# The modulation vectors of a hybrid block: column groups of TensorE in place of VectorE products

## The chip, the cores and the metric

The kernel runs on one core of one Trainium2 chip. The metric is the device time of one execution in microseconds (us); three executions of the kernel before took 2481.51 to 2481.74 us, with a median of 2481.51.

## The reference

One block of a transformer-like model works on 2048 latent tokens of 1024 features and on 256 context tokens:

```python
m_lat = silu(c) @ w_mod + b_mod            # (6*1024,), from one vector c
m_ctx = silu(c_ctx) @ w_mod + b_mod        # only its first two parts are used here
sh1, sc1, g1, sh2, sc2, g2 = split(m_lat, 6)
h_lat = rmsnorm(x, norm1) * (1 + sc1) + sh1       # h_ctx: the same with m_ctx
z = h_lat @ w_in                                  # 1024 -> 2336 columns
mix = concat(gated linear attention, RG-LRU, S5)(z) @ w_out
x = x + g1 * mix
h2 = rmsnorm(x, norm2) * (1 + sc2) + sh2
x = x + g2 * (relu(h2 @ w_ff1)**2 @ w_ff2)        # 1024 -> 4096 -> 1024
out = rmsnorm(x, final_norm)
```

The change is about the first two lines. `sh1` and `sc1` (and those of the context) are needed before any token can be projected; `g1`, `sh2`, `sc2` and `g2` are first needed by the output projection, much later. All arithmetic is in float32.

## The kernel before, in words

Features lie on the 128 partitions, tokens along the free axis, in four latent segments of 512 tokens and one context segment. Each large product is made of three matmuls on two fp32r parts of each operand (`mm3`, L323 to L326); the weights come in by DMA and are split by ScalarE (L319) and VectorE (L320).

The first phase (to about 850 us) has one main stream on TensorE, the input projection (`in_proj`), in the order: context, segments 0, 1, 3, 2, by groups of columns. Beside it run side streams: S5 (parameters, tables, then 16 groups one after another), the preparation of the attention blocks, the RG-LRU scans, the rest of the modulation vectors (`mod_rest`) and the first read-out. The class `Streams` decides the order in which the instructions are written: the main stream yields the time that each step takes, and a side stream gets a step when its own clock, scaled by a ratio, is behind. `mod_rest` yields 1.2 and has the ratio `RM` = 8, so that a step falls to every 9.6 units of the main stream (a unit is about a microsecond of matmuls). The framework then reorders the instructions by their dependences, their priorities and its own estimate of times, and fixes one order for each engine; each engine runs its list strictly in that order. The second phase (850 us to the end) is the MLP of the four segments, with the read-outs of the next segment beside it.

The modulation vectors are made in two places:

- `mod_first` (L246 to L272), at the very start. The first 2048 columns of `w_mod` come in by eight DMAs of 1 MB (L255), one for each 128 rows. `ct_` holds silu of c and of c_ctx, two columns for each of eight slices k of the features. For each k, four matmuls (L262) with those two columns as the stationary operand take 512 weight columns each to four PSUM banks, on partitions 0 and 1. ScalarE copies each bank to SBUF (L266), sixteen small transposes (L268) bring the result onto the partitions, and VectorE adds the bias (L269, L270) and makes `gsc1` (L271, L272).
- `mod_rest` (L274 to L281), beside the main stream. For each of the 32 remaining pieces of 128 outputs: one DMA of 512 KB of the transposed weights into the single buffer `wm` (L277), one VectorE product with silu(c), which `silu_c` (L240 to L244) had spread over all partitions, summed along the free axis (L278), and one small add of the bias (L279). The next DMA waits until the product has read the buffer.

In PSUM, the pool `acc` has two banks (main accumulators), `sa` three (S5 in the first phase), `sb` two and `mm` one.

Of the kernel before, what the change touches and what calls it, by code (L numbers as in the profile page):

```python
# [8 lines left out]
F32 = mybir.dt.float32  # L9
# [3 lines left out]
OP = mybir.AluOpType  # L13
# [5 lines left out]
KT = 8  # L19
# [4 lines left out]
NS = 16          # S5 groups  # L24
T8 = 8           # tokens that share a column of the S5 input layout
T16 = 16         # S5 chunk
NCH = SEQ // T16  # latent chunks
CCH = CTX // T16  # context chunks
NP = T16 + 2     # powers of the transition
XSZ = 1312  # L30
PKW = 1408       # S5 matrices of a group: read-out 2 x 256, input 4 x 128, kernel 3 x 128
# [11 lines left out]
# columns of the packed per-feature vector table  # L43
# [9 lines left out]
# W_in column tiles of 128 features  # L53
COLS = ["su0", "su1", "lx0", "lx1", "k0", "k1", "q0", "q1", "gg0", "gg1", "gg2", "gg3", "lg0", "lg1"]
WIDX = {n: i for i, n in enumerate(COLS)}
VN = 272         # half of v and the decay ranks of one direction


class Streams:
    """Emits a main and several side streams of instructions in step.  # L60

    A stream yields the time that its step takes, or the name of an event that has to be emitted first."""
# [10 lines left out]
    def step(self, limit):  # L73
        """One step of the side stream that is furthest behind; False if none is ready before `limit`."""
        ready = [x for x in self.live if (x[3] is None or x[3] in self.done) and (limit is None or x[2] <= limit)]
        if not ready:
            return False
        x = min(ready, key=lambda y: y[2])
        x[3] = None
        try:  # L80
            r = next(x[0])
        except StopIteration:
            self.live.remove(x)
            return True
        if isinstance(r, str):
            x[3] = r
        else:
            x[2] += r * x[1]
        return True

    def run(self, main):
        """`main` with the side streams."""
# [26 lines left out]
def hybrid_block(ctx: ExitStack, tc: tile.TileContext, xT, ctxT, cc, cct, wmodA, wmodT, pv, win, wva, wvb, upw, lrini, lruw, s5v, gluw,  # L119
# [27 lines left out]
    # ---------------------------------------------------------------- constants  # L147
# [14 lines left out]
    gsc1 = consts.tile([P, 16], F32, name="gsc1")      # norm1*(1+sc1): latent, context  # L162
    gsc2 = consts.tile([P, 8], F32, name="gsc2")

    # DRAM scratch, one tile per token segment
# [22 lines left out]
    qq_d = dram.tile([8, P, 1024], F32, name="qq_d")      # by pairs of blocks  # L188
    kk_d = dram.tile([8, P, 1024], F32, name="kk_d")
    ds_d = dram.tile([NB, 64, 512], F32, name="ds_d")      # backward block updates  # L190
    sf_d = dram.tile([16, 64, 512], F32, name="sf_d")      # forward states that enter the blocks
    bs_d = dram.tile([64, 512], F32, name="bs_d")          # backward state carried to the next segment
    # constant rows and borders of the scratch
# [7 lines left out]
    # ---------------------------------------------------------------- pools of the first phase  # L201
# [4 lines left out]
    def slots(tag, size, bufs):  # L206
        """A rotating workspace of `bufs` slots of `size` floats a partition."""
# [19 lines left out]
    def big_pair():  # L227
        """The two parts of a split operand of 512 tokens."""
        return [big.tile([P, KT, SEG], F32R, name=n, tag=n, bufs=2) for n in ("hH", "hL")]
# [3 lines left out]
    # ---------------------------------------------------------------- adaLN vectors  # L233
# [3 lines left out]
    # silu(c) on every partition, for the products that run along the free axis  # L237
    cbl = ip.tile([P, D], F32, name="cbl")

    def silu_c():  # L240
        S.dma_start(cbl, bass.AP(tensor=cc.tensor, offset=cc.offset, ap=[[0, P], [1, D]]))
        sgm = ip.tile([P, D], F32, name="sgm", tag="wm", bufs=MB)
        A.activation(sgm, cbl, AF.Sigmoid)
        V.tensor_tensor(cbl, cbl, sgm, OP.mult)  # L244

    def mod_first():  # L246
        """shift and scale of the first norm, latent and context"""
        wm = []
        with tc.high_priority(MF):
# [8 lines left out]
            V.tensor_tensor(ct_, ct_, csg, OP.mult)  # L258
        ms = [sa_tile(), sa_tile(), sb_tile(), sb_tile()]
        for k in range(KT):  # L260
            for j in range(4):
                T.matmul(ms[j][0:2, :], ct_[:, k, :], wm[k // 2][:, k % 2, j * 512:(j + 1) * 512], start=k == 0, stop=k == KT - 1)  # L262
        pt = acc_tile()[:, 0:32].rearrange("p (a b) -> p a b", b=2)
        for j in range(4):
            e = ip.tile([2, 512], F32, name="me", tag="ev", bufs=EV)
            A.copy(e, ms[j][0:2, :])  # L266
            for i in range(4):
                T.transpose(pt[:, 4 * j + i, :], e[:, i * P:(i + 1) * P], ident[0:2, 0:2])  # L268
        V.tensor_tensor(modl[:, 0:16], pt[:, :, 0], col("bmod", 0, 16), OP.add)  # L269
        V.tensor_tensor(modc, pt[:, :, 1], col("bmod", 0, 16), OP.add)  # L270
# [3 lines left out]
    def mod_rest(pool, j0, j1, tag="wm", bufs=MB):  # L274
        for j in range(j0, j1):
            wm = pool.tile([P, D], F32, name="wm", tag=tag, bufs=bufs)
            S.dma_start(wm, wmodT[(j - 16) * P:(j - 15) * P, :])  # L277
            V.scalar_tensor_tensor(wm, wm, 1.0, cbl, OP.mult, OP.mult, accum_out=modl[:, j:j + 1])  # L278
            V.tensor_tensor(modl[:, j:j + 1], modl[:, j:j + 1], col("bmod", j), OP.add)  # L279
            yield 1.2  # L280
        done.add("mod")  # L281

    # ---------------------------------------------------------------- normalized, modulated, split input
    def hprep(pool, src, t0, n, hH, hL, gsc, sh):
        """Normalize and modulate n tokens of src and split them exactly into two fp32r parts."""
        x = pool.tile([P, KT, n], F32, name="x", tag="x", bufs=XB)
        S.dma_start(x, src[:, t0:t0 + n].rearrange("(k p) t -> p k t", p=P))
        # 1/rms over the features on every partition
# [20 lines left out]
    def wsplit(pool, src, shape, tag, bufs, parts=None):  # L309
        """Load a weight tile and split it exactly into two fp32r parts (in `parts`, if they are there already);  # L310
        bufs: of the load, of each part."""
# [16 lines left out]
    # ---------------------------------------------------------------- input projection  # L328
# [40 lines left out]
    def v_cols(c, chunks):  # L369
        """Half of the values, token by token, with the decay ranks of one direction."""  # L370
# [50 lines left out]
    # ---------------------------------------------------------------- RG-LRU  # L421
# [21 lines left out]
    def lru(d, order, wl=wl):  # L443
        for s in order:
# [31 lines left out]
            # gates; sigmoid(z) = (1 + tanh(z/2))/2  # L476
# [35 lines left out]
    # ---------------------------------------------------------------- S5  # L512
# [4 lines left out]
    def s5_params():  # L517
# [73 lines left out]
        def cmul(or_, oi, ar, ai, br, bi, t, conj_b=False, neg_i=False):  # L591
            """(or, oi) = a*b (conj(b) if conj_b); oi negated if neg_i."""
# [51 lines left out]
        # step[k] = e^{+-i theta T 2^k}: + on the forward half, - on the backward half  # L644
# [7 lines left out]
        # input matrix  # L652
# [20 lines left out]
        # powers by slot: E: forward j, backward 17-j;  F: forward 15-s, backward s  # L673
# [13 lines left out]
    def s5_prep(b):  # L687
# [5 lines left out]
        # C lambda^k by slot  # L693
# [22 lines left out]
        # intra-chunk kernel, both directions  # L716
# [11 lines left out]
        # shifted windows of it make the Toeplitz blocks  # L728
# [9 lines left out]
    def s5_tables(g0):  # L738
        """Phase tables of four groups by doubling."""
# [23 lines left out]
    def s5_run(g):  # L763
# [32 lines left out]
        # real scans; results shifted by one chunk so that a chunk's column holds the state that enters it  # L796
# [9 lines left out]
        # the state that enters latent chunk c sits at column c + CCH + 1 on both halves  # L806
# [25 lines left out]
    # ---------------------------------------------------------------- GLA, first part: decays and block states  # L832
# [18 lines left out]
    def gla_prep(s, blocks, other=False):  # L851
        """Decays, decayed queries and keys, block updates, forward states of pairs of blocks of a segment.

        other: in the memory that the input's norm has left."""
# [15 lines left out]
        for b in blocks:  # L870
# [19 lines left out]
            # -log_sigmoid(z) = max(-z, 0) + log(1 + exp(-|z|))  # L890
# [49 lines left out]
            # forward states  # L940
# [16 lines left out]
    def gla_ends():  # L957
        """-log_sigmoid of the (shifted) token past the end of each sequence"""
# [15 lines left out]
    # ================================================================ read-out and MLP  # L974
# [15 lines left out]
    def ws(s, n, tag="t"):  # L990
        """Workspaces of the read-out, n tiles of 512; the last segment's come before the MLP's memory is there."""
# [11 lines left out]
    def decays():  # L1003
        # exponents of the decay between a block's anchor and the state that enters it
        # forward: -c_mid/16; backward: -(c_127 - c_mid + c_0 of the next block)/16
# [14 lines left out]
    def back_step(ss, blk):  # L1020
        """backward state that enters latent block blk -> ss[64:128]"""
# [17 lines left out]
    def open_ff():  # L1039
        """The first phase's workspaces make room for the MLP's."""  # L1040
# [8 lines left out]
    def read_out(s):  # L1049
        """Read-out of the three groups of a segment."""  # L1050
# [6 lines left out]
        # GLA read-out, pairs of blocks from the last to the first as the backward state runs  # L1057
# [55 lines left out]
        # RG-LRU gate  # L1113
# [14 lines left out]
        # S5 gate  # L1128
# [315 lines left out]
```

## Time and profile before

| | |
|---|---|
| median of three runs | 2481.51 us |
| profiled execution, first to last instruction | 2482.1 us |
| TensorE (PE) busy | 2347.2 us, 95% |
| PE weight loads (PEld) busy | 1886.0 us, 76% |
| VectorE (DVE) busy | 1610.0 us, 65% |
| ScalarE (ACT) busy | 1169.2 us, 47% |
| mean granted TensorE clock | 0.980 of full speed |

The page of the profile gives the profiled execution's span alone and nothing of what lies around it; the span is 0.6 us above the median. An fp32 matmul stands in the trace as two records and an fp32r matmul as one. The records' ends are modelled, so the pace of matmuls is read from their starts. Matmuls on fp32r operands are shown with the type f32 as well.

### The profile page before, as it was taken

To read this page: it belongs to the slowest core of one execution; us is meant where nothing else is said; L and a number is where in the kernel's file an instruction comes from. 1 tells how busy PE (TensorE), PEld (TensorE's weight loads), DVE (VectorE), ACT (ScalarE), POOL (GpSimd) and SP (SyncE) were. 2 spreads that over 40 slices of the span, in tenths; PEclk is the share of its full clock that TensorE was granted. 3 is DMA by queue.
4 is the path that set the end of the run, shared out by engine and by line. 5 is a ranking of instruction groups with operands and counts; after the bars stand their busy time and mean duration, and the time that the engine had idled before them with its cause. 6 is when DMAs were issued, how large, how long until landed. Compare 5 with 4: busy or idle time off the path is not lost.

```text
span 2482.1 us, 29891 instructions
## 1 busy us (share of the span) xinstructions
PE 2347.2 (95%) x10992; PEld 1886.0 (76%) x10992; DVE 1610.0 (65%) x2698; ACT 1169.2 (47%) x1704; POOL 100.7 (4%) x141
## 2 busy tenths in 40 slices
PE   7779999898887899999999999999999999999997
PEld 3668777877675677888877788887778888888886
DVE  6886878726786766565576656557655655655555
ACT  3764567436555645343355534336543433433333
POOL 1020111002100000000000000000000000000000
PEclk9989999999998999999999999999999999999999
DMA  7666777557775643322355322336522232333221
GB/s 258 209 201 208 223 238 227 168 174 207 253 240 181 206 135 120 101 94 93 100 177 162 118 86 93 102 102 202 159 85 94 94 102 87 126 102 102 94 94 51
DMA packets 189107, 364.03 MB, mean 147 GB/s; under 512 B 35200, under 2 KB 104144, under 8 KB 187920
## 3 DMA queue, kind: packets, MB, share of 16 engines
q1 hardware_dynamic: 183872, 346.20, 44.1%
q0 software_dynamic: 5088, 15.93, 1.9%
q8 instruction: 86, 1.41, 0.2%
q14 instruction: 61, 0.50, 0.1%
HBM read 299.76 MB, written 62.75 MB: 146 GB/s over the span
## 4 chain that ended last, share of the span: by engine, by line
PE 64%; ACT 5%; DVE 5%; DMA 3%; issue 2%; SPq 1%; POOL 0%; DVEq 0%; ACTq 0%; POOLq 0%
PE acc L324 10%; PE acc L326 9%; PE acc L325 9%; PE sa L324 9%; PE sa L325 9%; PE sa L326 9%; PE sb L324 2%; PE sb L326 2%; PE sb L325 2%; DVE wL L320 1%; ACT wH L319 1%; PE sb L1146 1%; DMA t<-lru 1%; DMA t<-kk_d 0%; DMA wR<-in_wout_dram 0%
## 5 line engine op out<-in xcount | busy, mean ns | idle before, releaser
L319 ACT CAST wH<-wR 128x1024 fp32r<-128x1024 f32 (+1 forms) x353 | 370.9, 1051 | 903.9 <-PE sa L325 432.8
L324 PE MATMUL acc<-hH,wH 128*128 128x512 f32 (+1 forms) x1576 | 629.6, 400 | 24.8 <-ACT hH L303 9.2
L320 DVE TENSOR_TENSOR wL<-wR,wH 128x1024 fp32r<-128x1024 f32 (+1 forms) x353 | 427.3, 1222 | 346.5 <-ACT wH L319 342.0
L326 PE MATMUL acc<-hH,wL 128*128 128x512 f32 (+1 forms) x1576 | 620.1, 394 | 3.2 <-DVE wL L320 3.1
L325 PE MATMUL acc<-hL,wH 128*128 128x512 f32 (+1 forms) x1576 | 617.7, 392 | 1.2 <-DVE hL L307 0.8
L1257 DVE SCALAR_TENSOR_TENSOR xa<-sa,modl,xa 128x512 f32<-128x512 f32 (+1 forms) x520 | 383.1, 741 | 197.5 <-PE sa L326 194.8
L324 PE MATMUL sa<-sH,wH 128*128 128x512 f32 (+1 forms) x1040 | 403.9, 389 | 4.6 <-DVE xa L1257 4.2
L326 PE MATMUL sa<-sH,wL 128*128 128x512 f32 (+1 forms) x1040 | 402.2, 387 | 0.0
L325 PE MATMUL sa<-sL,wH 128*128 128x512 f32 (+1 forms) x1040 | 401.9, 386 | 0.0
L324 PEld LDWEIGHTS acc<-hH,wH 128*128 128x128 f32 x1576 | 299.8, 191 | 95.3 <-ACT hH L303 10.3
L325 PEld LDWEIGHTS acc<-hL,wH 128*128 128x128 f32 x1576 | 300.1, 191 | 70.8 <-issue 6.2
L326 PEld LDWEIGHTS acc<-hH,wL 128*128 128x128 f32 x1576 | 299.5, 190 | 70.8 <-DVE wL L320 5.2
L324 PEld LDWEIGHTS sa<-sH,wH 128*128 128x128 f32 x1040 | 195.2, 188 | 49.2 <-DVE xa L1257 9.3
L326 PEld LDWEIGHTS sa<-sH,wL 128*128 128x128 f32 x1040 | 195.3, 188 | 40.8
L325 PEld LDWEIGHTS sa<-sL,wH 128*128 128x128 f32 x1040 | 195.4, 188 | 40.6 <-DVE sL L1233 0.8
L1233 DVE TENSOR_TENSOR sL<-sr,sH 128x512 fp32r<-128x512 f32 x128 | 88.2, 690 | 27.6 <-ACT sH L1232 27.5
L325 PE MATMUL acc<-wL,hH 128*128 128x272 f32 x288 | 87.8, 305 | 8.8 <-DVE wL L320 8.7
L324 PE MATMUL acc<-wH,hH 128*128 128x272 f32 x288 | 89.2, 310 | 2.0 <-ACT ev L331 1.9
L331 ACT COPY ev<-acc 128x512 f32<-128x512 f32 (+2 forms) x96 | 47.5, 495 | 85.1 <-issue 41.0
L326 PE MATMUL acc<-wH,hL 128*128 128x272 f32 x288 | 86.5, 301 | 0.0
L1232 ACT CAST sH<-sr 128x512 fp32r<-128x512 f32 x128 | 78.8, 617 | 10.8 <-PE sa L326 9.0
L1231 ACT ACTIVATE sr<-sr 128x512 f32<-128x512 f32 x128 | 80.8, 632 | 3.4
(402 smaller groups left out, 2717.2 us busy)
## 6 DMA issues: line engine op xcount, KB each, us to landing
wR<-in_w_dram SPq DMA_DIRECT2D x256, 512.0 KB
wR<-in_win_dram SPq DMA_DIRECT2D x54, 512.0 KB
wm<-in_wmodT_dram SPq DMA_DIRECT2D x32, 512.0 KB
wR<-in_wout_dram SPq DMA_DIRECT2D x32, 512.0 KB
wm<-in_wmodA_dram SPq DMA_DIRECT2D x8, 1024.0 KB
x<-in_xT_dram SPq DMA_DIRECT2D x8, 1024.0 KB
w<-pk_d SPq DMA_DIRECT2D x16, 512.0 KB
xa<-in_xT_dram SPq DMA_DIRECT2D x32, 256.0 KB
```

The costliest lines, as they stand in the source:

```text
L319: A.copy(Hf, raw)
L320: V.tensor_tensor(Lf, raw, f32(Hf), OP.subtract)
L324: T.matmul(acc, wH, hH, start=first, stop=False)
L325: T.matmul(acc, wH, hL, start=False, stop=False)
L326: T.matmul(acc, wL, hH, start=False, stop=last)
L331: A.copy(e, acc)
L1146: T.matmul(ps, gw[:, k, ct * P:(ct + 1) * P], sg[k], start=k == 0, stop=k == 1)
L1231: A.activation(r, r, AF.Square)
L1232: A.copy(sH, r)
L1233: V.tensor_tensor(sL, r, f32(sH), OP.subtract)
L1257: V.scalar_tensor_tensor(xa[:, m, a0:a1], acc, modl[:, 40 + m:41 + m], xa[:, m, a0:a1], OP.mult, OP.add)
```

## The change

The last four vectors go the way of the first two, and both ways put four results side by side in one bank. The columns of silu(c) and silu(c_ctx) are repeated 16 times, so that the stationary operand `c32[:, k]` has 32 columns; the matmul of the j-th group writes partitions 32j to 32j+31 (`tile_position` names that column group of the array). `mod_first` takes one bank of `sb` in place of two of `sa` and two of `sb`. `mod_rest` takes one bank of `sa` for each of two batches of 2048 columns, 16 steps each; a step loads 128 x 1024 weights, untransposed, into the same single buffer and runs two matmuls in two column groups. At the end of a batch `mod_columns` copies the bank, makes four full transposes into a bank of `acc`, and one VectorE add takes the 16 columns with the bias. `silu_c`, the broadcast load of c, `cbl`, the 32 products and the 32 small adds are gone. Comments are gone from the source as well, which moves line numbers.

```diff
-    cbl = ip.tile([P, D], F32, name="cbl")
-    def silu_c():
-        S.dma_start(cbl, bass.AP(tensor=cc.tensor, offset=cc.offset, ap=[[0, P], [1, D]]))
-        sgm = ip.tile([P, D], F32, name="sgm", tag="wm", bufs=MB)
-        A.activation(sgm, cbl, AF.Sigmoid)
-        V.tensor_tensor(cbl, cbl, sgm, OP.mult)
+    c32 = ip.tile([P, KT, 16, 2], F32, name="c32")
+    def mod_group(ms, k, j, w_):
+        T.matmul(ms[32 * j:32 * (j + 1), :], c32[:, k].rearrange("p a b -> p (a b)"), w_, start=k == 0, stop=k == KT - 1,
+                 tile_position=(0, 32 * j))
+    def mod_columns(ms):
+        pt = acc_tile()
+        e = ip.tile([P, 512], F32, name="me", tag="ev", bufs=EV)
+        A.copy(e, ms)
+        for i in range(4):
+            T.transpose(pt[:, i * P:(i + 1) * P], e[:, i * P:(i + 1) * P], ident)
+        return pt.rearrange("p (i j r) -> p j i r", i=4, j=4)
...
-            V.tensor_tensor(ct_, ct_, csg, OP.mult)
-        ms = [sa_tile(), sa_tile(), sb_tile(), sb_tile()]
+            V.tensor_tensor(c32, ct_.unsqueeze(2).to_broadcast([P, KT, 16, 2]), csg.unsqueeze(2).to_broadcast([P, KT, 16, 2]), OP.mult)
+        ms = sb_tile()
         for k in range(KT):
             for j in range(4):
-                T.matmul(ms[j][0:2, :], ct_[:, k, :], wm[k // 2][:, k % 2, j * 512:(j + 1) * 512], start=k == 0, stop=k == KT - 1)
...
+                mod_group(ms, k, j, wm[k // 2][:, k % 2, j * 512:(j + 1) * 512])
+        pt = mod_columns(ms)
...
-    def mod_rest(pool, j0, j1, tag="wm", bufs=MB):
-        for j in range(j0, j1):
-            wm = pool.tile([P, D], F32, name="wm", tag=tag, bufs=bufs)
-            S.dma_start(wm, wmodT[(j - 16) * P:(j - 15) * P, :])
-            V.scalar_tensor_tensor(wm, wm, 1.0, cbl, OP.mult, OP.mult, accum_out=modl[:, j:j + 1])
-            V.tensor_tensor(modl[:, j:j + 1], modl[:, j:j + 1], col("bmod", j), OP.add)
-            yield 1.2
+    def mod_rest():
+        for b in range(2):
+            ms = sa_tile()
+            for k in range(KT):
+                for j in range(2):
+                    wm = ip.tile([P, D], F32, name="wm", tag="wm", bufs=MB)
+                    S.dma_start(wm, wmodB[k * P:(k + 1) * P, (2 * b + j) * D:(2 * b + j + 1) * D])
+                    for i in range(2):
+                        mod_group(ms, k, 2 * j + i, wm[:, i * 512:(i + 1) * 512])
+                    yield 1.2
+            pt = mod_columns(ms)
+            V.tensor_tensor(four(modl[:, 16 * (b + 1):16 * (b + 2)]), pt[:, :, :, 0], four(col("bmod", 16 * (b + 1), 16)), OP.add)
         done.add("mod")
...
-    silu_c()
-    st.add(mod_rest(ip, 16, 48), RM)
+    st.add(mod_rest(), RM)
```

## Rows read from the trace of the kernel before

**Rows 1.** Part 1 of the page: busy time, share of span, instructions.

```profile
PE 2347.2 (95%) x10992; PEld 1886.0 (76%) x10992; DVE 1610.0 (65%) x2698; ACT 1169.2 (47%) x1704; POOL 100.7 (4%) x141
```

**Rows 2.** Windows: stretch, length, busy by engine (instructions), clock, DMA share, GB/s.

```profile
46.00:186.00 140.00, 111.01 (x579) 90.62 (x580) 123.87 (x286) 96.49 (x161) 20.05 (x21) 0.89 0.63 198
186.00:310.00 124.00, 117.74 (x690) 99.28 (x688) 89.45 (x169) 58.89 (x95) 12.91 (x19) 0.99 0.70 215
310.00:505.00 195.00, 180.49 (x972) 146.48 (x971) 147.28 (x290) 119.61 (x190) 26.81 (x33) 0.95 0.69 211
505.00:850.00 345.00, 297.27 (x1468) 236.94 (x1466) 227.69 (x445) 191.82 (x306) 31.72 (x48) 0.95 0.69 211
850.00:2482.00 1632.00, 1608.49 (x7210) 1305.64 (x7208) 996.79 (x1313) 690.18 (x939) 3.71 (x6) 1.00 0.35 112
```

**Rows 3.** Single lines: count, ns min/median/max, first and last start, shapes.

```profile
L278 DVE SCALAR_TENSOR_TENSOR wm<-wm,cbl x32: 1196/1218/1227, 79.4 to 502.5; 128x1024 f32<-128x1024 f32 x32
L278 DVE DVE_READ_ACCUMULATOR wm<-wm,cbl x32: 70/82/85, 80.5 to 503.6; 128x1 f32 x32
L279 DVE TENSOR_TENSOR modl<-modl,pvt x32: 132/151/161, 81.2 to 504.9; 128x1 f32<-128x1 f32 x32
L244 DVE TENSOR_TENSOR cbl<-cbl,sgm x1: 1217/1217/1217, 54.7 to 54.7; 128x1024 f32<-128x1024 f32 x1
```

**Rows 4.** Timeline of PE at the start: start, us, instruction, [idle before <- releaser].

```profile
17.49 1.88 PE L262 MATMUL sa<-wm,ct__146 128*2 128x512 f32 x4
...
39.81 1.88 PE L262 MATMUL sb<-wm,ct__146 128*2 128x512 f32 x4
...
43.09 0.70 PE L296 MATMUL mm<-ssum,ones 128*128 128x256 f32 x2
47.43 0.73 PE L324 MATMUL acc<-hH,wH 128*128 128x256 f32 x2 [3.65 <-ACT hH L303]
```

**Rows 5.** Timeline of the DMA queue of SyncE at the start.

```profile
28.91 0.34 SPq L841 DMA_DIRECT2D upt<-in_upw_dram  x1
```

**Rows 6.** Waits of that queue to 46 us: who for whom, us, times, longest.

```profile
SPq L841 <- DMA wm<-in_wmodA_dram: 1.1, 1, 1.1
```

**Rows 7.** Timeline of DVE at the start.

```profile
36.32 0.68 DVE L294 TENSOR_TENSOR ssum<-ssum 128x512 f32<-128x512 f32 x1
...
40.71 1.23 DVE L320 TENSOR_TENSOR wL<-wR,wH 128x1024 fp32r<-128x1024 f32 x1 [3.62 <-ACT wH L319]
...
41.93 0.42 DVE L294 TENSOR_TENSOR ssum<-ssum 128x256 f32<-128x256 f32 x1
```

**Rows 8.** Waits of PE from 46 to 186 us, the three longest tied to DVE.

```profile
PE acc L324 <- ACT hH L303: 9.2, 2, 5.6
PE acc L325 <- DVE wL L320: 7.8, 3, 5.4
...
PE mm L296 <- DVE ssum L294: 3.7, 1, 3.7
```

**Rows 9.** Timeline of PE: fp32 matmuls of 64 rows inside the stream.

```profile
850.45 0.40 PE L324 MATMUL acc<-hH,wH 128*128 128x512 f32 x1
850.78 0.48 PE L1078 MATMUL sb<-t 64*128 64x128 f32 x2
851.20 0.51 PE L325 MATMUL acc<-hL,wH 128*128 128x512 f32 x1
851.54 0.40 PE L326 MATMUL acc<-hH,wL 128*128 128x512 f32 x1
851.78 0.39 PE L324 MATMUL acc<-hH,wH 128*128 128x512 f32 x1
...
855.01 0.37 PE L1078 MATMUL sb<-t 64*128 64x128 f32 x1
855.02 0.37 PE L1079 MATMUL sb<-t 64*128 64x128 f32 x1
```

**Rows 10.** Waits of DVE from 186 to 505 us, the longest.

```profile
DVE wm L278 <- DMA wm<-in_wmodT_dram: 26.2, 11, 4.4
```

More of the change, by code (lines that the diff above doesn't have):

```diff
@@ L118, in hybrid_block @@
 @with_exitstack
-def hybrid_block(ctx: ExitStack, tc: tile.TileContext, xT, ctxT, cc, cct, wmodA, wmodT, pv, win, wva, wvb, upw, lrini, lruw, s5v, gluw,
+def hybrid_block(ctx: ExitStack, tc: tile.TileContext, xT, ctxT, cct, wmodA, wmodB, pv, win, wva, wvb, upw, lrini, lruw, s5v, gluw,
                  wout, w1, w2, cst, out, dbg=None):
@@ L236, in hybrid_block, with four @@
     csg = consts.tile([P, KT, 2], F32, name="csg")
-    cbl = ip.tile([P, D], F32, name="cbl")
-    def silu_c():
-        S.dma_start(cbl, bass.AP(tensor=cc.tensor, offset=cc.offset, ap=[[0, P], [1, D]]))
-        sgm = ip.tile([P, D], F32, name="sgm", tag="wm", bufs=MB)
-        A.activation(sgm, cbl, AF.Sigmoid)
-        V.tensor_tensor(cbl, cbl, sgm, OP.mult)
+    c32 = ip.tile([P, KT, 16, 2], F32, name="c32")
[9 more added lines that the diff above has]
+        return pt.rearrange("p (i j r) -> p j i r", i=4, j=4)
+    def four(t):
+        return t.rearrange("p (j i) -> p j i", j=4)
     def mod_first():
@@ L263, in mod_first @@
[L263 to L270, printed above, removed]
+                mod_group(ms, k, j, wm[k // 2][:, k % 2, j * 512:(j + 1) * 512])
@@ L271, in mod_first @@
+        pt = mod_columns(ms)
+        V.tensor_tensor(four(modl[:, 0:16]), pt[:, :, :, 0], four(col("bmod", 0, 16)), OP.add)
+        V.tensor_tensor(four(modc), pt[:, :, :, 1], four(col("bmod", 0, 16)), OP.add)
         V.scalar_tensor_tensor(gsc1[:, 0:8], modl[:, 8:16], 1.0, col("norm1", 0, 8), OP.add, OP.mult)
         V.scalar_tensor_tensor(gsc1[:, 8:16], modc[:, 8:16], 1.0, col("norm1", 0, 8), OP.add, OP.mult)
-    def mod_rest(pool, j0, j1, tag="wm", bufs=MB):
-        for j in range(j0, j1):
-            wm = pool.tile([P, D], F32, name="wm", tag=tag, bufs=bufs)
-            S.dma_start(wm, wmodT[(j - 16) * P:(j - 15) * P, :])
-            V.scalar_tensor_tensor(wm, wm, 1.0, cbl, OP.mult, OP.mult, accum_out=modl[:, j:j + 1])
-            V.tensor_tensor(modl[:, j:j + 1], modl[:, j:j + 1], col("bmod", j), OP.add)
-            yield 1.2
+    def mod_rest():
[10 more added lines that the diff above has]
+            V.tensor_tensor(four(modl[:, 16 * (b + 1):16 * (b + 2)]), pt[:, :, :, 0], four(col("bmod", 16 * (b + 1), 16)), OP.add)
@@ L1357, in pack @@
     r["ctxT"] = c_(a["ctx"][0].T)
-    r["cc"] = c_(np.concatenate([a["c"], a["c_ctx"][None]], 0))
-    r["cct"] = c_(r["cc"].reshape(2, KT, P).transpose(2, 1, 0).reshape(P, 16))
+    cc = np.concatenate([a["c"], a["c_ctx"][None]], 0)
+    r["cct"] = c_(cc.reshape(2, KT, P).transpose(2, 1, 0).reshape(P, 16))
     r["wmodA"] = c_(a["w_mod"][0][:, :2 * D])
-    r["wmodT"] = c_(a["w_mod"][0][:, 2 * D:].T)
+    r["wmodB"] = c_(a["w_mod"][0][:, 2 * D:])
     sgn = np.ones((P, 1), f4)
@@ L1422, in pack @@
     return {n: v.astype(f4, copy=False) for n, v in r.items()}
-_INS = ["xT", "ctxT", "cc", "cct", "wmodA", "wmodT", "pv", "win", "wva", "wvb", "upw", "lrini", "lruw", "s5v", "gluw", "wout", "w1", "w2", "cst"]
+_INS = ["xT", "ctxT", "cct", "wmodA", "wmodB", "pv", "win", "wva", "wvb", "upw", "lrini", "lruw", "s5v", "gluw", "wout", "w1", "w2", "cst"]
 def kernel(**inputs):
```

## The prediction

> **What bounds the kernel now.** I read part 1 of the page first: TensorE (PE) is busy 95% of the span, VectorE (DVE) 65%, ScalarE 47% [rows 1]. An average hides stages, so I read the windows next. From 850 us to the end PE is busy 1608 of 1632 us at full clock; that part is bound by PE, and the change does not touch it. Before 850 us the picture is mixed [rows 2]. From 46 to 186 us PE is busy 111 of 140 us at a mean clock of 0.89 while DVE is busy 124 (88%): PE stalls, DVE hardly does. From 186 to 310 us it is the other way round, PE 118 of 124 and DVE 89. From 310 to 505 us PE has 180 of 195, DVE 147. From 505 to 850 us PE is busy 297 of 345, but the modulation work is over by then, since its last product begins at 502.5 us [rows 3]. So the change takes work from the engine that is short only between 46 and 186 us and gives it to the engine that is short in the rest of its range. PE's idle time where it can be filled is 29.0 us (46 to 186) and 6.3 + 14.5 = 20.8 us (186 to 505), 49.8 us in all.
>
> **The start (faster).** The 64 fp32 records of the first two vectors run at an even pace: 13 groups of four records from 17.49 to 39.81 us are 1.72 us each, 0.43 us a record and 0.86 us for one 512-column matmul of two records [rows 4]. The eighth load of weights landed at 28.9 us, because SyncE's issue at that time had been waiting 1.1 us for such a load [rows 5, 6]. Before, then, PE and not the load ends this step. If four column groups run at once, 8 x 0.86 = 7 us of matmuls go with the loads, and the sum is there near 28.9 + 0.9 (at half clock 1.8), the copy and four transposes some 2 us later. What ends last then is the normalization of the context tokens. Its last add starts at 41.93 us, behind a weight split at 40.71 us that waits for ScalarE [rows 7], which had sat behind the copies out of PSUM. With those copies early, it follows the add at 36.32 us (0.68 us long): 36.9 + 0.42 = 37.4 us for the matmul with ones that ran at 43.09 us [rows 4]. The first projection moves with it, from 47.43 us. I take 5.7 us off. Bounds: 0 where the groups don't run together, and 10 us (38.8 to 28.9, where loads alone would set it). The larger stationary operand costs nothing: it is made while the first load is awaited.
>
> **What DVE loses.** 32 products of 1.22 us, the reading of the sum (0.08) and the add (0.15): 1.45 us each, 46.4 us; and the product of `silu_c`, 1.22 us [rows 3], which stands in the stretch that DVE sets, so 1.2 us off. The 32 products are spread over 423 us, so about 8 fall before 186 us: 11.6 of DVE's 123.9 us there. PE's waits in that stretch that DVE ends, directly or through ScalarE's `hH`, which is fed by DVE, are 9.2 + 7.8 + 3.7 = 20.7 us [rows 8]; each is followed by a stretch at half clock, 0.11 x 140 = 15.4 us of clock lost there [rows 2]. So the gain lies between 0 and 36 us. Eleven microseconds of DVE work can't buy much more than itself, and some of the stalls come before the first product at 79.4 us: I take 8. After 186 us DVE has room, and I take nothing.
>
> **What PE gains, the pairs.** 32 steps add two fp32 matmuls of 512 columns each. The trace of before has no column groups; the nearest are fp32 matmuls of 64 rows, which use half of the array, put into the main stream [rows 9]. They show two things. First, matmuls on the two halves start together (855.01 and 855.02 us). Second, leaving and entering the full array costs something. From the main matmul at 850.45 to the one at 851.54 us pass 1.09 us, with one matmul of two records (128 columns, 0.21 us at the pace above) between; two main matmuls take 2 x 0.23 us (851.54 to 851.78, shortened by rounding), so the insertion cost 0.63 us, 0.42 more than its work. A step therefore costs 0.86 + 0.42 = 1.28 us if the pair runs together and 1.72 + 0.42 = 2.14 if not: 41.0 or 68.5 us. I take 41.0, as the row halves behave so. The lower bound of a step is 0.86 (no switch), 27.5 us in all.
>
> The Trainium skill, "TensorE: Matmul & The Clock Gate", section "Part 3: Packing small matmuls — row/col tiling", gives 2.38 times for three column tiles, 0.79 of full overlap. By it a pair would take 1.72 / 1.59 = 1.08 us instead of 0.86, an estimate, and the sum would be 7 us higher. The halves in the trace lose nothing like it, but they are rows and not columns.
>
> **Where pairs hide.** The single buffer lets one pair follow the other only after a load, so a long stall of PE takes in one pair. PE's order is fixed from estimates, and a pair is a filler: it runs in a gap that the estimates see, or when its turn comes. I take 8 of the 32 in stalls that remain, 8 x 1.28 = 10.2 us off. Bounds: 0, and all of them.
>
> **Small parts.** The two batches end with a copy, four transposes (4 x 0.21 us) and one add each; the transposes' bank is one of the two main accumulators, and its hold should end within the 5.5 us that the other one is filled (24 x 0.23): 2 us together, bounds 2 and 10. One of three `sa` banks is held for most of 46 to 505 us; S5's preparation has two left, and its work is far from the path until its runs begin. A new wait comes with the pair: it waits for its load on PE, with the main matmuls queued behind it. DVE waited for these loads 26.2 us in 11 cases [rows 10]. There the products ran ahead of their turn, as soon as DVE had room, and so met loads just issued. On PE main matmuls are ready most of the time, and a pair mostly comes when its turn does, long after the load: I take 2 us, bounds 0 and 26.2. The loads' sizes and queue stay the same, with 4 KB a row.
>
> **The sum.** -5.7 - 1.2 - 8 + 41.0 - 10.2 + 2 + 2 = +19.9 us. Nothing behind 505 us gives it back: the S5 groups start when the last segment's columns are projected, and the MLP follows them. 2482.1 + 19.9 = 2502.0 for the span; the median of the runs lies 0.6 below the span, so 2501.4.
>
> **The rivals.**
>
> *DVE held PE (faster).* From 46 to 186 us DVE's busy share is higher than PE's. If every wait there goes, with the lost clock, 36 us come back instead of 8: -5.7 - 1.2 - 36 + 41.0 - 10.2 + 4 = -8.1, 2473 us. It decides from the point where DVE's relief before 186 us gives back more than 28 us. For it: 88% against 79%. Against: only 11.6 us of DVE's work go there, and ScalarE's evictions end some waits too.
>
> The Trainium skill, "Trainium Kernel Development and Optimization", section "Best Practices", says to judge the engine by the share of weight loads and not of matmuls. By that PE's 76% leaves room for every pair. But from 186 to 310 us, where PE is idle only 6.3 of 124 us, the loads' share is 99.28 of 124, 80% [rows 2]: a full stretch reads 80% by that measure, and 76% is near it.
>
> *Half of it (no change).* If DVE's relief is worth 22 us and 12 pairs hide, the sum is +0.8 us, about 2482.
>
> *Column groups run one after another.* Then the start gains nothing and a step costs 2.14 us: -1.2 - 8 + 68.5 - 8 x 2.14 + 4 = +46.2, 2528 us. For it: no column group was seen in this trace. Against: the row halves.
>
> *The wait for the loads moves to PE.* 26.2 instead of 2 us: +44.1, 2526 us. For it: rows 10, and one buffer. Against: PE is rarely idle from 186 to 310 us, where most of these waits must lie.
>
> **Chances.** The sum as made 0.42 (its own range 2488 to 2513); groups one after another 0.15; wait for loads 0.08; no change 0.11; DVE held PE 0.24. A difference under 0.2% (5 us) can't be told from none. Slower 0.65, the same 0.11, faster 0.24. The range, 2467 to 2540, takes in the faster case with a few microseconds to spare and both dear ones with their transposes at the upper bound.
>
> **What would show it.** The start: the first projection near 42 us instead of 47.4, and four matmuls on one bank starting within some 0.1 us of each other. Pairs: two matmuls starting together, and main matmuls on both sides 1.7 us apart for 1.28 us added; 2.6 us would say one after another. The waits of PE on loads of `wm`: near 2 us or near 26. PE's waits on the weight splits and on `hH` from 46 to 186 us: 20.7 us before; if they fall under 8 with the clock above 0.95, the faster rival holds. PE's busy time to 850 us should grow by about 20 us net of the first step. I am wrong if the projection of the last segment ends earlier than before, or if more than half of the pairs stand in idle time.

## The result, and the profile after

The changed kernel takes 2505.8 us (median of 4 runs, 2502.08 to 2508.37) against 2481.62 us (4 runs, 2481.51 to 2481.87): ratio 1.0098, 95% interval 1.0085 to 1.0111. It is slower by 24.2 us; 2501.4 was forecast. The total hides terms that were wrong in both directions, and they are the subject of what follows.

Part 1 of the page after, against [rows 1]. TensorE is busy 20.1 us longer (2347.2 to 2367.3), VectorE 35.9 us less:

```profile
PE 2367.3 (94%) x11116; PEld 1880.5 (75%) x11116; DVE 1574.1 (63%) x2603; ACT 1164.2 (46%) x1702; POOL 85.4 (3%) x141
```

The windows after, in the stretches and columns of [rows 2]:

```profile
46.00:186.00 140.00, 121.65 (x622) 91.74 (x621) 116.04 (x255) 93.73 (x157) 13.97 (x21) 0.90 0.65 202
186.00:310.00 124.00, 120.19 (x689) 94.08 (x688) 62.54 (x113) 53.44 (x87) 10.17 (x18) 1.00 0.54 163
310.00:505.00 195.00, 180.06 (x940) 134.02 (x940) 136.08 (x246) 118.11 (x189) 24.23 (x36) 0.97 0.73 224
505.00:850.00 345.00, 300.58 (x1530) 238.85 (x1527) 217.70 (x438) 176.22 (x289) 27.74 (x48) 0.95 0.67 207
```

PE is busier in the first stretch (121.65 against 111.01 us), and VectorE's load falls in the second from 89.45 to 62.54, in a stretch that PE sets. In the main stream PE now carries the work that these lines show (the view of one tile, the load target `wm`; columns as in [rows 3]):

```profile
L242 PE MATMUL sa<-wm,c x128: 592/617/1062, 47.2 to 531.1; 128*32 128x512 f32 x128
L242 PE MATMUL sb<-wm,c x64: 592/1060/1062, 11.3 to 30.5; 128*32 128x512 f32 x64
```

The timeline of PE after, in pieces: the start (against [rows 4]), one pair inside the 512-column stream, and the first matmul of the second phase, which begins with the MLP of the first segment; behind it the same matmul in the kernel before.

```profile
11.27 1.93 PE L242 MATMUL sb<-wm,c 128*32 128x512 f32 x8 [11.27 <-DVE w L595]
...
27.05 1.06 PE L242 MATMUL sb<-wm,c 128*32 128x512 f32 x8 [0.76 <-DMA wm<-in_wmodA_dram]
29.62 1.93 PE L242 MATMUL sb<-wm,c 128*32 128x512 f32 x8 [1.50 <-DMA wm<-in_wmodA_dram]
36.22 1.08 PE L251 MATMUL acc<-ident,me 128*128 128x128 f32 x4 [4.66 <-DMA ident<-in_cst_dram]
39.36 1.22 PE L308 MATMUL mm<-ssum,ones 128*128 128x256 f32 x2 [2.06 <-DVE ssum L306]
44.02 0.80 PE L336 MATMUL acc<-hH,wH 128*128 128x256 f32 x2 [3.44 <-ACT hH L315]
...
256.80 0.39 PE L337 MATMUL acc<-hL,wH 128*128 128x512 f32 x1
257.03 0.39 PE L338 MATMUL acc<-hH,wL 128*128 128x512 f32 x1
257.35 1.05 PE L242 MATMUL sa<-wm,c 128*32 128x512 f32 x4
258.33 0.50 PE L336 MATMUL acc<-hH,wH 128*128 128x512 f32 x1
258.67 0.39 PE L337 MATMUL acc<-hL,wH 128*128 128x512 f32 x1
...
867.54 1.22 PE L336 MATMUL acc<-hH,wH 128*128 128x512 f32 x2 [6.27 <-ACT hH L1213]
```

```profile
842.72 1.22 PE L324 MATMUL acc<-hH,wH 128*128 128x512 f32 x2 [6.27 <-ACT hH L1201]
```

Read the start first: eight records (four matmuls of two passes) are one group of 1.06 us at 27.05, where the granted clock is full, and of 1.93 us at 29.62, where it is half; the old start took 1.88 us for four records at full clock. The column groups do run together, and each group now waits for its load. The first projection comes at 44.02 instead of 47.43 us, 3.4 us earlier. The pair: from the main matmul at 257.03 to the second one behind it, 258.67, pass 1.64 us; without a pair two steps are 2 x 0.23. The pair costs 1.18 us. (In this trace 28 of the 32 pairs stand whole; four were split by the fixed order, their two matmuls apart, so that there are 36 insertions. A matmul alone pays as much: the one at 521.24 us also has 1.64 us from main matmul to main matmul.) Last, 867.54: before, the same matmul began at 842.72 us, and from there to the end both kernels take as long (2482.1 - 842.7 = 1639.4 us before, 2506.3 - 867.5 = 1638.8 after), with the same matmuls in the same order. So the whole loss, 24.8 us, lies ahead of that matmul, and 28.2 us of it behind the first projection.

The waits of PE from 46 to 186 us, against [rows 8] (who for whom, us, times, longest):

```profile
PE sa L242 <- DMA wm<-in_wmodB_dram: 6.7, 2, 4.2
...
PE acc L336 <- ACT hH L315: 2.1, 1, 2.1
...
PE acc L337 <- DVE wL L332: 1.1, 1, 1.1
...
PE mm L308 <- DVE ssum L306: 0.5, 1, 0.5
```

The three waits that were 20.7 us are 3.7. In their place stands one that was not there, for the loads of modulation weights; from 186 to 545 us it takes another 6.1 us in 6 cases, 12.8 in all.

### The profile page after: what moved, and what is told of

It reads as the page before. It is cut to its first block, busy times and chain, and to the rows that moved or that the text cites. A ratio compares the mean times of both kernels' runs of the same rounds, so it can differ in the third digit from the quotient of the medians.

```text
span 2506.3 us, 30026 instructions
## 1 busy us (share of the span) xinstructions
PE 2367.3 (94%) x11116; PEld 1880.5 (75%) x11116; DVE 1574.1 (63%) x2603; ACT 1164.2 (46%) x1702; POOL 85.4 (3%) x141
## 4 chain that ended last, share of the span: by engine, by line
PE 75%; ACT 8%; DVE 7%; DMA 6%; issue 3%; SPq 0%; POOL 0%; DVEq 0%; ACTq 0%; POOLq 0%
PE acc L336 12%; PE acc L338 12%; PE acc L337 12%; PE sa L336 9%; PE sa L337 9%; PE sa L338 9%; PE sb L336 2%; PE sb L338 2%; PE sb L337 2%; DVE wL L332 1%; ACT wH L331 1%; PE sa L242 1%; DMA wm<-in_wmodB_dram 1%; DMA x<-in_ctxT_dram 1%; PE sb L907 1%
## 5 line engine op out<-in xcount | busy, mean ns | idle before, releaser
L1244 ACT CAST sH<-sr 128x512 fp32r<-128x512 f32 x128 | 78.9, 617 | 10.8 <-PE sa L338 9.0
```

What stands on the lines that cost most here:

```text
L1244: A.copy(sH, r)
```

## The experiments

Each ran beside the kernel before on its chip, whose median there was 2479.5 to 2481.4 us; so ratios are compared, and "by ratio" means (ratio - 1) x 2481.6 us. Three questions were put: what each half of the change is worth (the first five), whether pairs and their loads are paid on the path (the next four), and why two kernels lost in a phase that they don't touch (the last three).

**The new start alone**, with the old products on VectorE for the last four vectors:

```diff
...
-    st.add(mod_rest(), RM)
+    silu_c()
+    st.add(mod_rest(ip, 16, 48), RM)
```

> The new first step (four column groups) with the 32 products of the last four vectors left on VectorE. The theory that the pairs of matmuls on TensorE are the whole loss, and that the start by itself gains what the trace shows at the first projection (47.4 to 44.0 us): 2478 us, between 2475 and 2480. The rival that the loss comes from the new start (half clock from 29 to 50 us, transposes that wait for the identity): 2490 us or more.

2476.83 us (10 runs), ratio 0.9981 [0.9971, 0.9991]: 4.7 us faster, the fastest kernel here that computes all six vectors. The first projection stands at 44.5 us and the second phase at 834.5.

**The pairs alone**, with the start of before:

```diff
+            V.tensor_tensor(ct_, ct_, csg, OP.mult)
...
-                mod_group(ms, k, j, wm[k // 2][:, k % 2, j * 512:(j + 1) * 512])
+                T.matmul(ms[j][0:2, :], ct_[:, k, :], wm[k // 2][:, k % 2, j * 512:(j + 1) * 512], start=k == 0, stop=k == KT - 1)
...
```

> The old first step (two columns, four banks) with the last four vectors in pairs on TensorE. The theory that the pairs are the loss and the start a gain of 3.4 us: 2509 us, between 2505 and 2513. The rival that the start carries the loss: 2485 us or less. If the two parts don't add up (this and the other half against the whole by more than 4 us), the order of work is the cause and not a price.

2513.48 us, ratio 1.0132 [1.0117, 1.0147]. This run is spoilt by its own edit: the product of c and its sigmoid slipped behind other work on VectorE, and PE's first matmul began at 21.56 us (a wait for that product) instead of 11.4; the first projection came at 56.5 us. It was repeated with the product in its place:

```diff
...
+            V.tensor_tensor(ct_, ct_, csg, OP.mult)
+            V.tensor_copy(c32, ct_.unsqueeze(2).to_broadcast([P, KT, 16, 2]))
...
```

> The old start (the vectors of the first norm as two-row matmuls one after another, in three banks) with the new pairs of the last four vectors, the product c times its sigmoid placed first on VectorE as before, and its 32-column copy taken behind it. If the parts add: the changed kernel less the gain that the new start alone gave, 3.4 us to the first projection and 4.6 us in time, so 2509 us (2505 to 2513), first projection at 47.5 us. Rival (the new start gives nothing of its own once the pairs follow): 2506 us. If the late first projection of the earlier kernel of this kind was not that product's place: 2513 us again with the first projection at 56 us.

2508.11 us, ratio 1.0113 [1.0096, 1.013], first projection at 46.55 us. The parts add: the pairs alone cost 28 us by ratio, the start alone gives 4.7, the sum is 23.3 against the 24.2 measured.

**The changed kernel without its pairs**: the last four vectors are left out, ones stand for them.

```diff
-    st.add(mod_rest(), RM)
+    V.memset(modl[:, 16:48], 1.0)
```

> The changed kernel without the last four vectors: their loads, matmuls, copies and transposes are left out, and ones stand in their place. It shows what the pairs and their loads cost as a whole. The theory that the pairs' time (32 times 1.2 us and 13 us of waits for loads) lies on the path: 2506 less 30 to 45, so 2461 to 2476 us. The rival that they are mostly hidden and the loss is a changed order: 2490 us or more.

2476.81 us, ratio 0.9976 [0.9963, 0.9988]. Against the changed kernel's 1.0098 the last four vectors cost 0.0122 x 2481.6 = 30.3 us, the low end of the 30 to 45 expected.

**The kernel before without its products**, with the same vectors left out:

```diff
-    silu_c()
-    st.add(mod_rest(ip, 16, 48), RM)
+    V.memset(modl[:, 16:48], 1.0)
```

> The kernel before without the last four vectors: their loads, the 32 products and adds, and the spreading of silu(c) are left out, and ones stand in their place. It shows what VectorE's relief is worth without any price on TensorE. My theory (8 us before 186 us, 1.2 for silu): 2473 us, between 2468 and 2479. The rival that VectorE held TensorE: 36 us or more come back, 2446 us or less. A third, that the products were wholly hidden: 2481 us.

2479.62 us, ratio 0.9998 [0.9988, 1.0007]. Products, sums and loads of those vectors together were worth 0.5 us, 3 at most. Its trace has the second phase at 837.6 us, 5.1 earlier than the trace of the kernel before; but that one seems to be of a longer execution, since its span lies 0.6 us above the median time, where the span of every other kernel here lies 1.8 to 2.2 us below the time of the same execution. VectorE's 88% from 46 to 186 us was no bound on the time. Its windows, in the columns of [rows 2], say how that can be: VectorE stays as busy (122.02 against 123.87 us), since other work moves up, and PE is busy 4.5 us longer, at a clock of 0.87 instead of 0.89. The three waits of [rows 8] fall from 20.7 us to 10.3 (3.6, 1.8 and 4.9), but others stand there instead, the longest 5.1 us.

```profile
46.00:186.00 140.00, 115.55 (x603) 96.11 (x604) 122.02 (x275) 98.81 (x165) 14.59 (x21) 0.87 0.58 178
186.00:310.00 124.00, 120.05 (x687) 100.92 (x687) 63.16 (x109) 56.55 (x91) 10.97 (x19) 0.97 0.50 148
```

**Each pair run twice**, the sum halved:

```diff
-                    for i in range(2):
-                        mod_group(ms, k, 2 * j + i, wm[:, i * 512:(i + 1) * 512])
+                    for n in range(2):
+                        for i in range(2):
+                            ... mod_group of 2 * j + i, accumulating over n
```

> The changed kernel with every pair of the last four vectors run twice (the bias add halves the sum). Work without a new switch, load or wait: 32 times 0.86, 27.5 us more on TensorE. If a pair's time lies on the path in full: 2533 us. If pairs hide as the whole change suggests (29 us of loss for 38 of pairs and 13 of waits, 57%): 2521 us. If they stand in idle time: 2508 us or less.

2532.45 us, ratio 1.0217 [1.0193, 1.024]. The timeline of PE, one doubled pair in the same surroundings:

```profile
265.89 0.39 PE L341 MATMUL acc<-hH,wL 128*128 128x512 f32 x1
266.21 1.91 PE L291 MATMUL sa<-wm,c 128*32 128x512 f32 x8
268.05 0.50 PE L339 MATMUL acc<-hH,wH 128*128 128x512 f32 x1
268.39 0.40 PE L340 MATMUL acc<-hL,wH 128*128 128x512 f32 x1
```

From 265.89 to 268.39 are 2.50 us against 1.64: a second pair adds 0.86, so 0.32 of the 1.18 us belongs to going over to the column groups and back. The Trainium skill, "TensorEngine Tiling (Array Packing)", section "Key Properties", says that a change of the tiling mode drains the engine; these rows agree in that the change has a price, 0.32 us for both ways (that a drain is what takes it, they do not show). Thirty-two second pairs are 27.5 us; by ratio this kernel is 29.5 us above the changed kernel. In the traces the second phase moves by 21.7 us, from 867.5 to 889.2. The windows of both from 46 us to there, first the changed kernel:

```profile
46.00:867.54 821.54, 733.35 (x3812) 565.32 (x3811) 541.32 (x1064) 454.51 (x736) 76.12 (x121) 0.95 0.66 204
46.00:889.23 843.23, 755.01 (x3939) 565.51 (x3938) 540.43 (x1061) 461.47 (x742) 80.89 (x121) 0.97 0.65 198
```

PE is idle 88.2 us in both (821.54 - 733.35 and 843.23 - 755.01): the waits for loads fall from 12.9 to 7.0 us, and other idle time grows by as much. So no part of the second pairs found idle time. That PE is busy only 21.7 us longer goes with the clock, 0.97 instead of 0.95. What is added to a pair is paid.

**Two buffers for the loads.** To make room the 32-column copies of c were replaced by a window that slides over one zero-padded row, and two 64-byte tiles left the pool of constants:

```diff
-RB, MB, XB, OW, MF, LI, GR = 2, 1, 1, 2, 5000, 3, 4
+RB, MB, XB, OW, MF, LI, GR = 2, 2, 1, 2, 5000, 3, 4
...
-    ct_ = consts.tile([P, KT, 2], F32, name="ct_")
-    csg = consts.tile([P, KT, 2], F32, name="csg")
+    ct_ = ip.tile([P, KT, 2], F32, name="ct_", tag="ssum")
+    csg = ip.tile([P, KT, 2], F32, name="csg", tag="sq")
...
-    c32 = ip.tile([P, KT, 16, 2], F32, name="c32")
+    c32 = ip.tile([P, KT + 15, 2], F32, name="c32")
...
```

> The changed kernel with two buffers for the loads of the last four vectors in place of one; to make room, the 32 stationary columns are a window over the eight pairs of columns and zeros. Takes away what makes the pairs wait for their loads (12.8 us in the trace of after). If these waits lie on the path: 2493 us, between 2490 and 2497. If they hide in other stalls: 2504 us or more.

2510.58 us, ratio 1.0125 [1.01, 1.015]. The waits fall to 3.4 us in 3 cases, and the second phase starts at 853.8 us, 13.7 earlier. But that phase then lasts 1650.7 us, 12 longer, though its matmuls are the same in the same order. So the total met neither expectation.

**One load for four groups**, 1 MB each, with the same memory edit:

```diff
-                for j in range(2):
-                    wm = ip.tile([P, D], F32, name="wm", tag="wm", bufs=MB)
...
+                wm = ip.tile([P, 2 * D], F32, name="wm", tag="wm", bufs=MB)
+                S.dma_start(wm, wmodB[k * P:(k + 1) * P, 2 * b * D:2 * (b + 1) * D])
+                for j in range(4):
+                    mod_group(ms, k, j, wm[:, j * 512:(j + 1) * 512])
```

> The changed kernel with loads of 1 MB and all four column groups at once in 16 steps (the same window for the stationary columns). If four run together as two do, 16 steps cost 0.86 + 0.32 us each, 19 us in place of 38: 2487 us, less if the waits shrink with the number of steps, 2492 if the longer loads add waits. If only two run together at a time: 2501 us or more.

2497.81 us, ratio 1.0073 [1.0052, 1.0094]. Second phase from 850.7 us, 1650.4 us long: again a gain ahead of it and 11 us lost in it, and a total that fits none of the expectations.

**The pairs later**, beside the S5 groups, where PE idles more [rows 2]:

```diff
-RX, RY, RZ, RM, RO, RO3, XR = 3.0, 0.8, 4.0, 8.0, 1.1, 0.7, 0.3
+RX, RY, RZ, RM, RO, RO3, XR = 3.0, 0.8, 4.0, 1.4, 1.1, 0.7, 0.3
...
+        yield "lx1_2"
```

> The changed kernel with the last four vectors begun after the last segment's columns for the RG-LRU are projected (ratio 1.4 in place of 8), beside the S5 groups, where TensorE idles 44 us. If pairs cost what they displace and idle time takes them in: 2490 us or less. If the S5 groups' matmuls queue behind pairs that wait for their loads, the chain of S5 gets longer: 2506 us or more.

2565.1 us, ratio 1.0342 [1.0315, 1.037], the worst of all. The longest waits of PE from 46 us to its second phase at 923.1:

```profile
PE sa L242 <- DMA wm<-in_wmodB_dram: 31.5, 18, 5.1
PE acc L337 <- ACT wH L332: 13.1, 5, 8.7
PE sb L941 <- issue: 11.2, 4, 5.3
PE sa L836 <- DVE w L827: 8.9, 7, 3.1
```

The window from 46 us to its second phase, against the changed kernel's 821.54 us above:

```profile
46.00:923.10 877.10, 755.04 (x3813) 584.50 (x3813) 543.43 (x1066) 458.67 (x739) 78.73 (x121) 0.92 0.63 191
```

Of the 55.6 us that the second phase comes later, 33.9 are idle time of PE (122.1 against 88.2 us), 18.6 of these its waits for loads. The other 21.7 us PE is busy longer with the same matmuls, at a clock of 0.92 instead of 0.95. PE's idle time there is no room. That the S5 steps on the other engines wait for PE in turn, and that each pair that waits for its load holds them up too, is the likely reason, but no run tests it.

**The place of the tiles alone.** The changed kernel, with the two 64-byte tiles moved out of the pool of constants and nothing else:

```diff
-    ct_ = consts.tile([P, KT, 2], F32, name="ct_")
-    csg = consts.tile([P, KT, 2], F32, name="csg")
+    ct_ = ip.tile([P, KT, 2], F32, name="ct_")
+    csg = ip.tile([P, KT, 2], F32, name="csg")
```

> The changed kernel with one edit: the two 64-byte tiles of c and of its sigmoid go from the pool of the constants into the pool of the first phase, so that every tile allocated behind the constants lies 128 bytes per partition lower. No instruction is added, removed or reordered. Theory (it is the place of the tiles that slowed the second phase of the two-buffer and the 1 MB kernels, 229.4 to 233.4 ns for a first MLP matmul): the first phase as in the changed kernel (second phase from 867 us), the second phase 1650 us instead of 1639, in all 2517 us (2514 to 2520). Rival (the narrow 46-column stationary tile, or the larger first-phase pool, did it): second phase 1639 us, in all 2506 us.

2521.5 us, ratio 1.0156 [1.0132, 1.0179], 14 us above the changed kernel by ratio. Groups of matmuls from 850 us to the end, first of the changed kernel, then of this one (line, tiles, shape, count, busy us, mean ns):

```profile
L336 PE MATMUL acc<-hH,wH 128*128 128x512 f32 x1033 | 415.1, 402 | 6.3 <-ACT hH L1213 6.3
L338 PE MATMUL acc<-hH,wL 128*128 128x512 f32 x1034 | 408.1, 395 | 0.0
...
L337 PE MATMUL acc<-hL,wH 128*128 128x512 f32 x1033 | 403.5, 391 | 0.0
```

```profile
L336 PE MATMUL acc<-hH,wH 128*128 128x512 f32 x1041 | 419.5, 403 | 6.3 <-ACT hH L1213 6.3
L338 PE MATMUL acc<-hH,wL 128*128 128x512 f32 x1041 | 413.2, 397 | 0.0
L337 PE MATMUL acc<-hL,wH 128*128 128x512 f32 x1041 | 411.6, 395 | 0.0
```

Records overlap, so their means show only part of it. From start to start, averaged over the second phase of each trace, the three kinds take 231.1, 229.3 and 227.2 ns in the changed kernel and 233.3, 233.4 and 233.3 here; the matmuls into `sa` keep their 227 to 228. Some 3650 matmuls (with those into `sb`) by 4.1 ns are 15 us, less 1 that `sa` gains; the second phase lasts 1651.5 us, 12.8 longer, and begins 5.5 us later. Which tile's address it is, and what about it, stays open.

**The 1 MB loads with the pool kept as large**: the window of c goes into the pool that the small tiles leave, so that the tiles behind it stay where they were.

```diff
-    modc = consts.tile([P, 16], F32, name="modc")
...
+    ct_ = ip.tile([P, KT, 2], F32, name="ct_", tag="ssum")
+    csg = ip.tile([P, KT, 2], F32, name="csg", tag="sq")
+    modc = ip.tile([P, 16], F32, name="modc")
...
+    c32 = consts.tile([P, KT + 16, 2], F32, name="c32")
...
```

> The 1 MB loads with four column groups at a time again, but with the pool of the constants as large as in the changed kernel, so that the tiles behind it keep their addresses. Placement theory: second phase from 850 us as before and 1639 us long, in all 2488 us (2485 to 2493). Rival (the second phase was slowed by something else in that kernel): second phase 1650 us, in all 2498 to 2501 us. If the price of the pairs on TensorE were what the four groups cannot lower, the second phase would begin at 860 us or later.

2487.64 us, ratio 1.0032 [1.0019, 1.0044], 16 us under the changed kernel by ratio. The second phase begins at 847.1 and lasts 1639.4 us. The timeline of PE:

```profile
316.11 0.40 PE L338 MATMUL acc<-hH,wL 128*128 128x512 f32 x1
316.44 1.06 PE L243 MATMUL sa<-wm,c 128*32 128x512 f32 x8
317.43 0.50 PE L336 MATMUL acc<-hH,wH 128*128 128x512 f32 x1
317.77 0.39 PE L337 MATMUL acc<-hL,wH 128*128 128x512 f32 x1
...
467.53 1.04 PE L243 MATMUL sa<-wm,c 128*32 128x512 f32 x2
...
468.96 1.06 PE L243 MATMUL sa<-wm,c 128*32 128x512 f32 x6
```

Four groups take 1.06 us where two took 1.05, and the step costs 317.77 - 316.11 - 0.46 = 1.20 us. But only nine of the 16 steps stand whole; the fixed order split seven into one matmul and three, as at 467.53, so that there are 23 insertions where the changed kernel has 36. At these prices, taken for every insertion, they are 27.6 us against 42.5; waits for loads are 4.3 us instead of 12.9. Of these 23.5 us the start of the second phase gains 20.4.

**Two buffers with the pool kept as large**, by the same memory edit as in the kernel just above:

```diff
-RB, MB, XB, OW, MF, LI, GR = 2, 1, 1, 2, 5000, 3, 4
+RB, MB, XB, OW, MF, LI, GR = 2, 2, 1, 2, 5000, 3, 4
```

> The changed kernel with two buffers for the modulation loads, pool of the constants kept as large as in the changed kernel. Theory (the waits for the modulation loads, 12.8 us in the changed kernel, lie on the path, and the later loss was one of placement): second phase from 854 us, 1639 us long, in all 2493 us (2490 to 2498). Rival (placement was not the cause): second phase 1650 us, 2505 us or more. Rival (the waits are hidden in later stalls): second phase from 865 us, 2504 us.

2501.82 us, ratio 1.008 [1.0055, 1.0105], with a wide spread (2493.58 to 2506.76). None of the three expectations was met. The first phase does what the theory says: waits of 3.2 us instead of 12.9, second phase from 858.4 us, 9.1 earlier, so most of the waits are on the path. The matmuls into `acc` keep the fast pace (227.1 ns from start to start for the kind with `hL`), so neither the larger pool of the first phase nor the sliding window is what slowed the two kernels above. But the phase lasts 1646.4 us in the profiled run, the slowest of the four. The waits of PE from 860 us on, longest first:

```profile
PE sa L337 <- DVE xa L1270: 6.3, 7, 3.0
```

In the changed kernel's trace they are 2.9 us in 6 cases, the longest 0.9. Behind the 3.0 us, near 1399 us, PE has 6.8 us at half clock that the changed kernel's trace does not have. Why that wait grew stays open.

## Why the forecast held, and which of its steps did not

The total was 4 us low, and the side was right. The side rests on the pairs, whose price was foreseen; that the total came so near is luck, since terms that were wrong by 9 to 13 us cancelled. By its own steps:

- *The start, -5.7.* The mechanism was right: four groups run together and the loads set their pace. Measured: 3.4 us at the first projection, 4.7 us in time with the old products kept. The error is in the 37.4 us for the matmul with ones: it ran at 39.36. The add that was to end at 36.9 (36.32 + 0.68 is 37.0) began 0.66 us later than before, and a second weight split went ahead of the last add on VectorE:

```profile
36.98 0.69 DVE L306 TENSOR_TENSOR ssum<-ssum 128x512 f32<-128x512 f32 x1
...
37.67 1.22 DVE L332 TENSOR_TENSOR wL<-wR,wH 128x1024 fp32r<-128x1024 f32 x1
...
38.89 0.42 DVE L306 TENSOR_TENSOR ssum<-ssum 128x256 f32<-128x256 f32 x1
```

From that matmul to the projection it took 0.3 us more than before (4.66 against 4.34), at half clock. The transposes, expected near 32 us, stand at 36.22 because they waited for the load of the identity; this cost nothing here, since what they give was ready at 40.1 us and first used at 42.95.
- *What DVE loses, -8 and the product of `silu_c`, -1.2.* This step failed. "Eleven microseconds of DVE work can't buy much more than itself" held only as an upper bound: all of it taken away buys 0.5 us. The waits of [rows 8] went away in the changed kernel, but pairs and their waits stand in their place, and in the kernel before without its products half of them went away and the time stayed.
- *A pair, 1.28 us.* Measured 1.18; the row halves in [rows 9] were a good model, with 0.32 for the switch where 0.42 was read. The estimate of 1.08 us for the pair's own work, from the 2.38 times for three column tiles in the Trainium skill ("TensorE: Matmul & The Clock Gate", section "Part 3: Packing small matmuls — row/col tiling"), is not borne out: a second pair costs 0.86, and a step of four groups 0.02 more than one of two.
- *The number of pairs.* The prediction took 32 insertions; the order made 36 of them, 42.5 us at 1.18 each, where 41.0 was forecast.
- *Hidden, 10.2.* Mis-sized. The kernel to compare with is the changed one without its pairs. Its window from 46 us to its second phase:

```profile
46.00:836.06 790.06, 697.23 (x3676) 566.74 (x3674) 539.16 (x1058) 458.01 (x737) 82.25 (x121) 0.94 0.62 191
```

PE is idle 92.8 us there, and 88.2 in the changed kernel. Without the 12.9 that are new, 75.3 of the old kind are left, so 17.5 us of pairs went into idle time, the worth of 15 of the 32; "more than half of the pairs", a sign set for being wrong, was near. The clock gave back some 5 us more, an estimate: in these stretches PE is busy at half clock for 68.8 us without the pairs and for 58.1 with them, by the granted clock laid over the busy time, and half of the difference is saved. Together that is some 23 us, more than twice the forecast, and the clock had no term in it.
- *Waits for the loads, 2.* Failed, towards the rival: 12.8. The argument was that a pair "mostly comes when its turn does, long after the load". But the waits of over 0.4 us came at pairs whose load had been issued only 4 to 8 us before; at 283.06 us, for instance, PE waited 2.1 us for a load issued at 277.53. A second buffer takes most of it away (3.2 us), though a load was also issued late, here 5 us after the pair before it had left the buffer. The waits are not the price of what is hidden: with two buffers and the pool kept as large PE is idle 82.1 us from 46 us to the second phase, 78.9 without its own waits for loads, so 14 us of pairs are still in idle time.
- *The sum with measured terms:* -4.7 - 0.5 + 42.5 - 22.8 + 12.8 and about 1 for two groups of transposes are +28.3; measured +24.2, so the terms are good to some 4 us. The errors cancelled: +8.7 in DVE's relief and the silu product, +1 at the start, +1.5 in the pairs and +10.8 in waits against -12.6 in hiding and -1 in the transposes.

Of the rivals, *groups one after another* is refuted by the rows at 29.62 and 257.35 us. *DVE held PE* is refuted by the kernel before without its products (3 us at most, where 28 were needed). *The wait moves to PE* is true for half of its price. *Half of it*: more than 12 pairs hide, but DVE's relief of 22 us is not there, so it did not come. Of the marks set beforehand, "waits under 8 with the clock above 0.95" is instructive: the waits did fall to 3.7, but the clock is 0.90 and the faster rival is wrong. Vanished waits alone prove no gain: here the waiting engine was given other work to do in them.

## What to carry to other kernels

A busy engine is not a bound: before pricing relief, take the work away once and see whether anything moves, as the kernel without its products did here. Work moved onto the engine that bounds the rest has to have its data there when its turn comes; feed it in few large steps, which pay for fewer switches and fewer waits (32 pairs cost 30 us, 16 fours some 16 us less), and look in the trace whether the steps stayed whole. And keep the half that stands on its own: the groups at the start, with the other four vectors left on VectorE, are the best version here, 4.7 us under the kernel before, though by less than the 5 us that was set as the limit of what a single comparison can tell.

## What the runs showed of the hardware that was not expected

- Matmuls on different column groups start 6 to 7 ns apart (257.35 us and its neighbours in the trace) and share their time in full: 1.04 us for one alone, 1.05 for two, 1.06 for four, each with two passes of 512 columns at full clock.
- Moving the tiles allocated behind the pool of constants down by 128 bytes per partition changed the pace of the full-array matmuls into `acc` and `sb` from 227 to 231 ns to some 233, with the same instructions in the same order, and cost 14 us. Three kernels with this shift have a second phase of 1650 to 1652 us; in the others, whose matmuls there are the same in the same order, it lasts 1638 to 1642 us, and 1646.4 in one with the fast pace. An experiment that frees a little memory can bring such a loss with it; with the size of the freed pool kept, the loss was gone (1639.4 us for the second phase).
